# Two column blocks held in PSUM over the first rounds, modulation pieces re-spaced, small vectors prepared in steps (hybrid decoder layer, one core)

## The chip, the core and the metric

One core of a Trainium2 chip runs the whole layer as one program. The metric is the device time of one execution in microseconds (us); the time before is the median of three runs. The engines named below are PE (TensorE, matrix products), DVE (VectorE), ACT (ScalarE), POOL (GpSimd) and SP (SyncE, which here issues nearly all loads). Every engine works through its own list of instructions in order.

## What is computed

One decoder layer for 256 tokens of width 2048, in float32. Only its first third matters here:

```python
mod = silu(c) @ w_ada + b_ada            # six vectors of 2048: sh1, sc1, gt1, sh2, sc2, gt2
h = rmsnorm(x, g_mix) * (1 + sc1) + sh1
z = h @ w_in                             # 2048 x 16392; split into mq mk mv mo, mi mf, dq dk dv, sq sk sv, gm gd gs
...                                      # mLSTM, differential attention, stick-breaking attention
x = x + gt1 * (merged @ w_out)
...                                      # second norm, gated MLP with a short convolution, residual with gt2
```

`w_ada` has 2048 rows and 12288 columns. The first two of its six column groups (sh1 and sc1, 33.6 MB) must be read and summed against `silu(c)` before the matching rows of `h` exist, so the first product `h @ w_in` cannot start all of its contraction at once.

## The kernel before, in words

**Products.** Every large product splits both factors into a high part (float32r) and a low rest and adds three products: high by high, low by high, high by low. A load from `w_in` of four contraction tiles (a tile is 128 rows; `kt` counts them, 16 in all) by 512 or 440 columns lands in `raw`; ACT copies the high part (`hi`, line 320), DVE subtracts to get the low part (`lo`, line 322), both on two tiles at a time, and PE then runs the matmuls of lines 352 (orientation T, tokens on the output's partitions, two outputs) or 354 (orientation F, features on the partitions, four outputs). The other factor is `hh`/`hl`, the two parts of `h`.

**The first rounds.** Thirteen column blocks (`first`: two each for sq, sk and sv, seven of 440 columns for the gates and dq, dk, dv) are computed in rounds over the contraction, because `h` becomes ready from the front: round 1 takes kt 0 to 1 of all blocks, round 2 kt 2 to 3, round 3 kt 4 to 7, round 4 kt 8 to 11 (of eleven blocks, `NE`), and round 5 the rest. `partial` (line 467) does one block of one round. Since a block's sum does not stay in PSUM between rounds, the two PSUM accumulators (`gp`, three buffers) are emptied after each block and round: by an ACT copy in round 1 (line 476), and by a DVE multiply-add onto the sum in SBUF in all later rounds (line 478).

**The modulation.** `ada_first` makes the pieces of sh1 and sc1 for kt 0 to 1 and then 2 to 3, `ada_quad` those for kt 4 to 7, 8 to 11 and 12 to 15 ("quads" below). Each step loads a piece of `w_ada` and adds it, weighted with a column of `silu(c)`, to an accumulator on DVE (`ada_mac`, lines 204 and 206; a quad has 8 steps of two 128x1024 operations). When all 16 row tiles are in, `ada_sums` sums over partitions by matmuls with a column of ones into the single bank of pool `adaps` (line 222), DVE makes `b1` and `a1` (lines 225 to 227), and `make_h` makes `hh` and `hl` from the normalised x (lines 415, 370, 371).

**What sets the order.** The steps are Python generators in two queues, `ada` and `side`. `tick` (line 191) adds a rate to a counter after each block and runs that many steps, so the rates 0.5, 0.45 and 0.63 place the modulation steps between blocks; before a block that needs rows of `h` that are not there yet, line 469 runs steps until they are. The framework's scheduler then orders each engine's list; `issue_after` adds an ordering constraint. SP's loads are one such list. Quads, `ada_first` and four-tile weight loads share the three buffers of `rawp`; two-tile weight loads use three buffers of `adap`. Pool `mx` has four PSUM banks, used here by `norm_x` for transposes at the start and by the attention steps from block 6 of round 5 on (line 808).

```python
    rates["ada"] = 0.5
    for ci in range(13):
        partial(ci, 0, 2)
    rates["ada"] = 0.45
    for ci in range(13):
        partial(ci, 2, 4)
    with tc.issue_after(state["load"].ins):
        late_vectors()
    rates["ada"] = 0.63
    for ci in range(13):
        partial(ci, 4, 8)
    for ci in range(NE):
        partial(ci, 8, 12)
    drain(ada)
```

**Small vectors.** `late_vectors` (line 135) loads 14 small pieces (gains, convolution taps, gate biases, lambda vectors; SP, lines 140 to 151), transposes them on PE into columns and works out lambda on DVE and ACT; here it stands as one piece between rounds 2 and 3. At the start, `silu(c)` and five bias and gain vectors are transposed into one bank `pc` (lines 116 and 117) and copied to `colsA`; `norm_x` (line 388) takes the square root of the mean square (line 393) and scales and transposes x.

Of the kernel before, what the change touches and what calls it, by code (L numbers as in the profile page):

```python
# [17 lines left out]
P = 128  # L18
# [3 lines left out]
KD = D // P  # L22
# [17 lines left out]
def kernel(  # L40
# [32 lines left out]
    def sidewide(name):  # L73
        return tmp.tile([P, 512], F32, tag="sidewide", name=name, bufs=4)
# [4 lines left out]
    V, A, T = nc.vector, nc.scalar, nc.tensor  # L79
# [32 lines left out]
    nc.scalar.dma_start(rowsA[16:48], b_rows[0:32])  # L112
    nc.scalar.dma_start(rowsA[48:80], b_rows[48:80])
    V.tensor_tensor(csig, csig, crow, ALU.mult)
    pc = bank("pc")
    T.transpose(pc[:, 0:KD], csig, ident[:KD, :KD])
    T.transpose(pc[:, KD:KD + 80], rowsA, ident[:80, :80])
    colsA = const.tile([P, KD + 80], F32, name="colsA")
    V.tensor_copy(colsA[:, 0:KD], pc[:, 0:KD])
    V.tensor_copy(colsA[:, KD:KD + 80], pc[:, KD:KD + 80])  # L120
    ccol, gmix_c = colsA[:, 0:16], colsA[:, 16:32]
    bsh1_c, bsc1_c, bsh2_c, bsc2_c = (colsA[:, 32 + 16 * i:48 + 16 * i] for i in range(4))
# [12 lines left out]
    def late_vectors():  # L135
        rows = slot(3, "rows2")
        rowsB, rowsC = rows[0:27, 0:P], rows[0:64, P:2 * P]
        rowsD = rows[0:NF, 2 * P:5 * P].rearrange("k (j p) -> k j p", j=3)
        ld = nc.sync.dma_start
        ld(rowsB[0:16], g_ffn[0].rearrange("(k p) -> k p", p=P))  # L140
        ld(rowsB[16:24], g_mout[0].rearrange("h (k p) -> (h k) p", p=P))
        ld(rowsB[24:25], g_dsub)
        for r in range(2):
            ld(rowsB[25:26, r * 64:(r + 1) * 64], g_dq)
            ld(rowsB[26:27, r * 64:(r + 1) * 64], g_dk)
        ld(rowsC, w_mconv[0].rearrange("j (k p) -> (j k) p", p=P))
# [12 lines left out]
        V.tensor_scalar(gdq_c, gdq_c, 64.0 ** -0.5, None, ALU.mult)

        lp = rows[0:1, 896:1024].rearrange("o (v d) -> o v d", v=2)
        V.tensor_tensor(lp, lamv[:, 0::2, :], lamv[:, 1::2, :], ALU.mult)
        ls = const.tile([1, 2], F32, name="ls")
        V.tensor_reduce(ls, lp, AX.X, ALU.add)
        A.activation(ls, ls, AF.Exp)
        nl = const.tile([1, 1], F32, name="nl")
        V.scalar_tensor_tensor(nl, ls[:, 1:2], -LAM_INIT, ls[:, 0:1], ALU.add, ALU.subtract)
        plam = bank("plam")
        T.matmul(plam[:, 0:1], lhsT=ones[0:1, :], rhs=nl, start=True, stop=True)
        V.tensor_copy(nlam, plam[:, 0:1])  # L170

# [14 lines left out]
    def drain(queue):  # L186
        pump(queue, 1 << 30)
# [42 lines left out]
    def ada_first(k0):  # L230

        accs = [adap.tile([P, 512], F32, tag="acc", name="acc", bufs=2)]
        if k0 == 0:
            accs.append(sidewide("acc2"))
        for q in range(4):
            raw = rawp.tile([P, 4, 512], F32, tag="raw", name="raw")
            step = 2 if k0 == 0 and q == 3 else 4
            for j in range(0, 4, step):
                for i in range(2):
                    r0, c0 = q * 512 + j * P, i * D + k0 * P  # L240
                    with tc.issue_after(state["load"].ins) if k0 else nullcontext():
                        load = nc.sync.dma_start(raw[:, j:j + step, i * 256:(i + 1) * 256],
                                                 w_ada[r0:r0 + step * P, c0:c0 + 256].rearrange("(k p) f -> p k f", p=P))
            if k0 == 0:
                state["load"] = load
            with tc.issue_after(state["first"].ins) if k0 == 2 and q == 0 else nullcontext():
                ada_mac(accs, raw, 4 * q, 4)
            yield
        ada_sums(accs, k0, 2)
# [75 lines left out]
            los.append(lo)  # L325
        return his, los

    def gemm(orient, act, W, row0, col0, n, kt0, kt1, hold=None, hold_all=False):

        acc = [gp.tile([P, 512], F32, tag="gp", name="gp") for _ in range(2)]
        ah, al = act
        started, left = set(), {}
        nt = 2 if orient == "T" else n // P
        per = 1 if orient == "T" else 2

        def mms(t, ks, s0, wh, wl):
            if orient == "T":
                o, sl = acc[t][:, :n], slice(t * P, (t + 1) * P)  # L340
            else:
                o, sl = acc[t // 2][:, (t % 2) * S:(t % 2 + 1) * S], slice(t * P, (t + 1) * P)
            for w, acts in ((wh, (ah, al)), (wl, (ah,))):
                for k in ks:
                    wk = w[k // 2][:, k % 2, :]
                    for a in acts:
                        b = t // per
                        start = b not in started
                        started.add(b)
                        kw = dict(start=start, stop=s0 + k == kt1 - 1 and w is wl, skip_group_check=True)  # L350
                        if orient == "T":
                            T.matmul(o, lhsT=a(s0 + k)[:, sl], rhs=wk[:, :n], **kw)  # L352
                        else:
                            T.matmul(o, lhsT=wk[:, sl], rhs=a(s0 + k), **kw)  # L354

        for s0 in range(kt0, kt1, 4):
            nk = min(4, kt1 - s0)
            r0 = row0 + s0 * P
            wh, wl = weights(W[r0:r0 + nk * P, col0:col0 + n], nk, n, hold if s0 > kt0 or hold_all else None)
            last = s0 + nk >= kt1  # L360
            for ks in ([range(nk)] if last else [range(k0, k0 + 2) for k0 in range(0, nk, 2)]):
                for t in range(nt):
                    mms(t, ks, s0, wh, wl)
            if not last:
                tick()
        return acc
# [87 lines left out]
    first = []  # L454
# [9 lines left out]
    def shaped(src, dst):  # L464
        return src.rearrange("p (a b) -> p a b", a=dst.shape[1]) if len(dst.shape) == 3 else src

    def partial(ci, kt0, kt1):
        orient, col0, n, dest, scale = first[ci]
        while state["h"] < kt1:
            pump(ada, 1)  # L470
        pin = kt0 == 0 and ci == 1
        acc = gemm(orient, hact, w_in, 0, col0, n, kt0, kt1, hold=state["first"] if pin else None, hold_all=pin)
        for b in range(2):
            for cs, d in dest(b):
                if kt0 == 0:
# [24 lines left out]

    def stick():
# [502 lines left out]
```

## Time and profile before

| | |
|---|---|
| median of three runs | 1848.84 us (1844.38 to 1850.06) |
| the profiled execution | 1845.87 us, of which the span from the first to the last instruction is 1844.2 us |
| PE, busy share of the span | 97% |
| PE weight loads | 92% |
| DVE | 71% |
| ACT | 48% |
| mean granted TensorE clock | 0.989 of full speed |
| bytes read from HBM | 419.68 MB |

The span is what the profile's stretches are counted in, from its own start; the time of an execution is 1.7 us longer. A busy PE may still run at half the clock or wait a little between matmuls, so the count of matmuls and their pace say more than the share.

### The profile page before, as it was taken

The numbers are of one execution on the slowest core, as the hardware profiler recorded it, in microseconds if no ns is written. First come the engines' busy times: TensorE is split into PE (matmuls) and PEld (weight loads), VectorE is DVE, ScalarE is ACT, GpSimd is POOL, SyncE is SP. The second block draws the span as 40 slices with busy tenths as digits, with TensorE's granted clock in tenths as the row PEclk, the third lists the DMA queues.
The fourth block names the chain that finished last, engine by engine and source line by source line (L and its number), as shares of the span: only waits on it lengthen the run. The fifth ranks groups of instructions, "written<-read, shape, count | busy, mean of one in ns | idle before, by whom it ended". The sixth has DMA issues, their size and how long they took to land.

```text
span 1844.2 us, 30193 instructions
## 1 busy us (share of the span) xinstructions
PE 1795.0 (97%) x12461; PEld 1689.7 (92%) x12461; DVE 1313.8 (71%) x1715; ACT 878.8 (48%) x1132; POOL 9.0 (0%) x30
## 2 busy tenths in 40 slices
PE   6979899999999999999999999999999999999998
PEld 5879889999978999999999889999998899999987
DVE  6988777888888587786887576777775545555554
ACT  7533334667455554543444464444443334444432
POOL 0000000000000000000000000000000000000000
PEclk9989899999999999999999999999999999999999
DMA  9978765666677567677887547777765555555563
GB/s 331 334 256 296 252 230 167 238 240 229 231 247 266 173 218 259 209 244 271 294 307 268 188 151 240 250 241 274 251 206 197 191 185 184 182 184 183 192 217 114
DMA packets 219655, 423.73 MB, mean 230 GB/s; under 512 B 8768, under 2 KB 31613, under 8 KB 219005
## 3 DMA queue, kind: packets, MB, share of 16 engines
q1 hardware_dynamic: 217693, 417.56, 67.1%
q8 instruction: 97, 1.59, 0.4%
q10 hardware_dynamic: 1280, 2.14, 0.3%
q0 software_dynamic: 544, 2.11, 0.3%
q14 instruction: 41, 0.34, 0.0%
HBM read 419.68 MB, written 2.10 MB: 229 GB/s over the span
## 4 chain that ended last, share of the span: by engine, by line
PE 92%; DVE 4%; DMA 2%; ACT 1%; issue 1%; SPq 0%; DVEq 0%; ACTq 0%
PE gp L354 60%; PE gp L352 28%; DVE lo L322 1%; DMA raw<-in_w_in_dram 1%; DMA raw<-in_w_ada_dram 1%; DVE quads L206 1%; PE psc L602 0%; DMA x<-in_x_dram 0%; ACT hi L320 0%; PE pxt L402 0%; ACT x L396 0%; PE px L910 0%; PE pr L299 0%; PE pm L212 0%; PE pdt L587 0%
## 5 line engine op out<-in xcount | busy, mean ns | idle before, releaser
L322 DVE TENSOR_TENSOR lo<-raw,hi 128x1024 fp32r<-128x1024 f32 (+1 forms) x608 | 728.6, 1207 | 367.6 <-ACT hi L320 345.5
L320 ACT CAST hi<-raw 128x1024 fp32r<-128x1024 f32 (+1 forms) x608 | 622.3, 1038 | 740.5 <-PE gp L354 393.0
L354 PE MATMUL gp<-hh,hi 128*128 128x256 f32 x2688 | 700.7, 286 | 21.3 <-ACT hh L370 18.1
L354 PE MATMUL gp<-hl,hi 128*128 128x256 f32 x2688 | 700.8, 285 | 0.2 <-DVE hl L371 0.2
L354 PEld LDWEIGHTS gp<-hh,hi 128*128 128x128 f32 x2688 | 520.2, 194 | 23.7 <-ACT hh L370 18.3
L354 PEld LDWEIGHTS gp<-hl,hi 128*128 128x128 f32 x2688 | 520.8, 194 | 0.9 <-DVE hl L371 0.5
L354 PE MATMUL gp<-hh,lo 128*128 128x256 f32 x2688 | 511.0, 284 | 0.5 <-DVE lo L322 0.5
L354 PEld LDWEIGHTS gp<-hh,lo 128*128 128x128 f32 x2688 | 406.9, 193 | 1.4 <-DVE lo L322 0.9
L206 DVE SCALAR_TENSOR_TENSOR acc<-araw,colsA,acc 128x512 f32<-128x512 f32 x240 | 179.0, 746 | 5.2 <-DMA araw<-in_w_ada_dram 3.2
L352 PE MATMUL gp<-hi,hh 128*128 128x440 f32 (+1 forms) x416 | 157.7, 379 | 4.1 <-DVE dq L478 1.7
L352 PE MATMUL gp<-hi,hl 128*128 128x440 f32 (+1 forms) x416 | 156.3, 376 | 0.0
L352 PE MATMUL gp<-hi,atl 128*128 128x512 f32 x352 | 136.9, 389 | 0.0
L352 PE MATMUL gp<-hi,ath 128*128 128x512 f32 x352 | 136.9, 389 | 0.0
L352 PE MATMUL gp<-lo,hh 128*128 128x440 f32 (+1 forms) x416 | 113.6, 376 | 0.0
L352 PE MATMUL gp<-lo,ath 128*128 128x512 f32 x352 | 105.7, 389 | 0.0
L352 PEld LDWEIGHTS gp<-hi,hh 128*128 128x128 f32 x416 | 78.2, 188 | 16.8 <-issue 5.2
L352 PEld LDWEIGHTS gp<-lo,hh 128*128 128x128 f32 x416 | 77.8, 188 | 11.0 <-issue 1.0
L352 PEld LDWEIGHTS gp<-hi,hl 128*128 128x128 f32 x416 | 78.2, 188 | 9.8
L352 PEld LDWEIGHTS gp<-lo,ath 128*128 128x128 f32 x352 | 66.1, 188 | 13.8
L352 PEld LDWEIGHTS gp<-hi,ath 128*128 128x128 f32 x352 | 66.1, 188 | 13.7
L352 PEld LDWEIGHTS gp<-hi,atl 128*128 128x128 f32 x352 | 66.1, 188 | 13.7
L206 DVE SCALAR_TENSOR_TENSOR quads<-raw,colsA,quads 128x1024 f32<-128x1024 f32 x45 | 57.5, 1278 | 12.3 <-DMA raw<-in_w_ada_dram 12.2
(332 smaller groups left out, 1584.8 us busy)
## 6 DMA issues: line engine op xcount, KB each, us to landing
raw<-in_w_in_dram SPq DMA_DIRECT2D x98, 1024.0 KB, 5.3
raw<-in_w_up_dram SPq DMA_DIRECT2D x88, 1024.0 KB, 5.0
araw<-in_w_ada_dram SPq DMA_DIRECT2D x128, 512.0 KB, 5.3
raw<-in_w_down_dram SPq DMA_DIRECT2D x44, 1024.0 KB, 5.0
raw<-in_w_ada_dram SPq DMA_DIRECT2D x62, 512.0 KB, 5.7
raw<-in_w_branch_dram SPq DMA_DIRECT2D x24, 1024.0 KB, 6.6
raw<-in_w_in_dram SPq DMA_DIRECT2D x21, 880.0 KB, 4.8
raw<-in_w_out_dram SPq DMA_DIRECT2D x16, 1024.0 KB, 4.9
```

The source lines that it names most:

```text
L206: V.scalar_tensor_tensor(acc, raw[:, k, :], ccol[:, kt:kt + 1], acc, ALU.mult, ALU.add)
L320: A.copy(hi[:, :, :n], raw[:, k0:k0 + 2, :n])
L322: state["split"] = V.tensor_tensor(lo[:, :, :n], raw[:, k0:k0 + 2, :n], hi[:, :, :n].bitcast(F32), ALU.subtract)
L352: T.matmul(o, lhsT=a(s0 + k)[:, sl], rhs=wk[:, :n], **kw)
L354: T.matmul(o, lhsT=wk[:, sl], rhs=a(s0 + k), **kw)
```

## The change

1. **Kept sums.** Blocks 0 and 1 (sq) get two banks each of pool `mx` in round 1 and accumulate in them through all five rounds; ACT copies them out once, at the end of round 5. `gemm` takes the accumulators as an argument.
2. **Rates.** The `ada` rate is 0.56 in rounds 1 and 2, 0.75 in round 3 and 0.86 in round 4.
3. **Small vectors in steps.** `late_vectors` has three `yield`s, runs from the `side` queue with rate 0.4 from round 3 on, uses the bank of `adaps` for its transposes and for lambda, and is no longer ordered behind a load.
4. **Start.** A one-element square root (`root`) stands ahead of the squares of x; `silu(c)` has a bank and a tile of its own (`ccol`) and is copied before the other vectors are transposed; `ada_first(0)` uses one accumulator in place of two.

```diff
+    root = const.tile([P, 1], F32, name="root")
+    A.activation(root, eps_c, AF.Sqrt)
+    pc, pg = bank("pc"), bank("pg")
     T.transpose(pc[:, 0:KD], csig, ident[:KD, :KD])
-    T.transpose(pc[:, KD:KD + 80], rowsA, ident[:80, :80])
...
+    V.tensor_copy(ccol, pc[:, 0:KD])
+    T.transpose(pg[:, 0:80], rowsA, ident[:80, :80])
...
+        yield
+        pv = adaps.tile([P, 512], F32, tag="adaps", name="pv")
...
+        yield
+        plam = adaps.tile([P, 512], F32, tag="adaps", name="plam")
...
-        if k0 == 0:
-            accs.append(sidewide("acc2"))
...
-    def gemm(orient, act, W, row0, col0, n, kt0, kt1, hold=None, hold_all=False):
+    def gemm(orient, act, W, row0, col0, n, kt0, kt1, hold=None, hold_all=False, acc=None):
+        started = set() if acc is None or kt0 == 0 else {0, 1}
+        if acc is None:
+            acc = [gp.tile([P, 512], F32, tag="gp", name="gp") for _ in range(2)]
...
+        if kt0 == 0 and ci < 2:
+            kept[ci] = [bank("kept"), bank("kept")]
...
+                if ci in kept:
+                    if kt1 == KD:
+                        A.activation(d, shaped(acc[b][:, cs], d), AF.Copy, scale=scale)
+                elif kt0 == 0:
...
-    rates["ada"] = 0.5
+    rates["ada"] = 0.56
     for ci in range(13):
         partial(ci, 0, 2)
-    rates["ada"] = 0.45
     for ci in range(13):
         partial(ci, 2, 4)
-    with tc.issue_after(state["load"].ins):
-        late_vectors()
-    rates["ada"] = 0.63
+    side.append(late_vectors())
+    rates["side"] = 0.4
+    rates["ada"] = 0.75
     for ci in range(13):
         partial(ci, 4, 8)
+    rates["ada"] = 0.86
     for ci in range(NE):
         partial(ci, 8, 12)
     drain(ada)
+    drain(side)
```

DVE at the end of round 3, before. `dv..<-gp` are the last blocks' multiply-adds, `quads` the modulation steps, `b1`/`a1` the results of the partition sums for kt 8 to 11, and `hl` the low part of `h` without which round 4 cannot go on.

```order
L478 SCALAR_TENSOR_TENSOR dv_255<-gp_1645,dv_255 128x440
L322 TENSOR_TENSOR lo_1762<-raw_1755,hi_1761 128x1024
L206 SCALAR_TENSOR_TENSOR quads_257<-raw4_1815,colsA_122,quads_257 128x1024
L478 SCALAR_TENSOR_TENSOR dv_255<-gp_1682,dv_255 128x440
L206 SCALAR_TENSOR_TENSOR quads_257<-raw4_1815,colsA_122,quads_257 128x1024
L478 SCALAR_TENSOR_TENSOR dv_255<-gp_1683,dv_255 128x440
L225 TENSOR_TENSOR b1_131<-pm_1720,colsA_122 128x4
L226 TENSOR_TENSOR a1_130<-pm_1720,colsA_122 128x4
L322 TENSOR_TENSOR lo_1825<-raw_1822,hi_1824 128x1024
L227 TENSOR_TENSOR a1_130<-a1_130,colsA_122 128x4
L322 TENSOR_TENSOR lo_1829<-raw_1822,hi_1828 128x1024
L371 TENSOR_TENSOR hl_135<-ht_1732,hh_134 128x256
```

Here `b1` comes after the last block of the round (`gp_1682`, `gp_1683`). The same engine and place in the change:

```order
L231 TENSOR_TENSOR b1_135<-pm_1542,colsA_127 128x4
L232 TENSOR_TENSOR a1_134<-pm_1542,colsA_127 128x4
L326 TENSOR_TENSOR lo_1626<-raw_1623,hi_1625 128x2x440
L326 TENSOR_TENSOR lo_1630<-raw_1623,hi_1629 128x2x440
L233 TENSOR_TENSOR a1_134<-a1_134,colsA_127 128x4
L489 SCALAR_TENSOR_TENSOR dk_253<-gp_1575,dk_253 128x440
L326 TENSOR_TENSOR lo_1666<-raw_1663,hi_1665 128x2x440
L489 SCALAR_TENSOR_TENSOR dk_253<-gp_1576,dk_253 128x440
L176 COPY nlam_133<-plam_1618 128x1
L212 SCALAR_TENSOR_TENSOR quads_256<-raw4_1699,ccol_124,quads_256 128x1024
L326 TENSOR_TENSOR lo_1670<-raw_1663,hi_1669 128x2x440
L376 TENSOR_TENSOR hl_139<-ht_1554,hh_138 128x256
```

Now `b1` stands before the multiply-adds of block 9 (`gp_1575`), and `hl` three blocks ahead of the round's last one; the copy of lambda (`nlam`) lies between.

DVE at the end of round 2 in the change, the sums for kt 4 to 7; `gp_1026` and `gp_1027` are the round's last block:

```order
L233 TENSOR_TENSOR a1_134<-a1_134,colsA_127 128x4
L489 SCALAR_TENSOR_TENSOR dv_254<-gp_999,dv_254 128x440
L326 TENSOR_TENSOR lo_1051<-raw_1048,hi_1050 128x1024
L489 SCALAR_TENSOR_TENSOR dv_254<-gp_1000,dv_254 128x440
L326 TENSOR_TENSOR lo_1055<-raw_1048,hi_1054 128x1024
L163 TENSOR_SCALAR cols_131<-cols_131 128x1
L164 TENSOR_SCALAR cols_131<-cols_131 128x1
L212 SCALAR_TENSOR_TENSOR quads_256<-raw4_1021,ccol_124,quads_256 128x1024
L489 SCALAR_TENSOR_TENSOR dv_254<-gp_1026,dv_254 128x440
L489 SCALAR_TENSOR_TENSOR dv_254<-gp_1027,dv_254 128x440
L376 TENSOR_TENSOR hl_139<-ht_978,hh_138 128x256
```

The sums are made earlier here too, but `hl` is written only after the round's last multiply-add.

SP's loads near the start of the change, with what each waits for (`DMAHW0` to `DMAHW7` are eight landing counters that the loads take in turn, so a load that waits for one waits for an earlier load to land). `raw_322` is the first modulation load for kt 2 to 3, `raw2_365` the weights of the fourth block, the `rows2` loads seven of the 14 small vectors:

```order
L246 DMA raw_322<-in_w_ada_dram 128x4x256 [waits DMAHW5_49]
L143 DMA rows2_1236<-in_g_ffn_dram 16x128 [waits DMAHW6_49,PE_49,Activation_49]
L144 DMA rows2_1236<-in_g_mout_dram 8x128 [waits DMAHW7_49]
L145 DMA rows2_1236<-in_g_dsub_dram 1x128 [waits DMAHW0_49]
L147 DMA rows2_1236<-in_g_dq_dram 1x64 [waits DMAHW1_49]
L148 DMA rows2_1236<-in_g_dk_dram 1x64 [waits DMAHW2_49]
L147 DMA rows2_1236<-in_g_dq_dram 1x64 [waits DMAHW3_49]
L148 DMA rows2_1236<-in_g_dk_dram 1x64 [waits DMAHW4_49]
L319 DMA raw2_365<-in_w_in_dram 128x2x512 [waits DMAHW5_49,DVE_49]
L246 DMA raw_397<-in_w_ada_dram 128x4x256 [waits DMAHW6_49]
```

Before, all 14 stood between rounds 2 and 3 and `raw_370`, the load of that fourth block, followed the modulation loads at once. Now thirteen of them stand in two batches (seven, shown, and six behind the next two modulation loads) ahead of the fifth block's weights, and one before them.

## Rows read from the trace of the kernel before

**Rows 1.** The page, part 1: busy time of each engine.
```profile
PE 1795.0 (97%) x12461; PEld 1689.7 (92%) x12461; DVE 1313.8 (71%) x1715; ACT 878.8 (48%) x1132; POOL 9.0 (0%) x30
```
**Rows 2.** Stretches (us): length, busy PE, PEld, DVE, ACT, POOL, clock, DMA share, GB/s.
```profile
26.30:67.00 40.70, 40.68 (x242) 38.71 (x243) 36.22 (x46) 28.53 (x51) 0.00 (x0) 0.93 1.01 345
67.00:107.30 40.30, 35.41 (x200) 30.16 (x198) 39.59 (x60) 11.49 (x13) 0.00 (x0) 1.00 0.83 283
107.30:114.45 7.15, 0.00 (x1) 0.00 (x1) 6.11 (x10) 5.82 (x9) 0.00 (x0) 0.71 0.99 327
114.45:186.90 72.45, 72.26 (x424) 67.97 (x424) 59.64 (x75) 23.93 (x28) 0.00 (x0) 0.96 0.84 283
186.90:193.63 6.73, 0.01 (x1) 0.00 (x0) 5.92 (x10) 3.92 (x7) 0.00 (x0) 0.64 0.81 275
193.63:256.10 62.47, 62.47 (x376) 58.88 (x376) 51.10 (x63) 22.41 (x26) 0.00 (x0) 0.96 0.77 266
256.10:260.35 4.25, 0.04 (x1) 0.00 (x0) 2.27 (x8) 1.93 (x5) 0.00 (x0) 0.62 0.78 256
```
**Rows 3.** Who PE waited for: us in total, times, longest.
```profile
PE gp L354 <- ACT hh L370: 18.1, 3, 7.2
```
**Rows 4.** Short stretches after the first and the third wait, columns as in rows 2.
```profile
116.00:120.00 4.00, 4.00 (x20) 4.00 (x20) 1.83 (x4) 0.63 (x2) 0.00 (x0) 0.50 0.99 331
260.00:264.00 4.00, 3.65 (x17) 3.65 (x18) 1.52 (x4) 1.82 (x6) 0.00 (x0) 0.51 0.60 225
```
**Rows 5.** The chain that ended last: start, us, what; PE's pace.
```profile
796.52 51.83 PE gp L354 x432
1369.58 130.57 PE gp L352 x576
```
**Rows 6.** Timeline of PE: start, us, what; two successive matmuls of 440 columns.
```profile
102.75 0.36 PE L352 MATMUL gp<-hi,hh 128*128 128x440 f32 x1
102.95 0.36 PE L352 MATMUL gp<-hi,hl 128*128 128x440 f32 x1
```
**Rows 7.** DVE by form, 20 to 260 us: count, busy, mean ns, idle before.
```profile
L206 DVE SCALAR_TENSOR_TENSOR quads<-raw,colsA,quads 128x1024 f32<-128x1024 f32 x45 | 57.5, 1278 | 12.3 <-DMA raw<-in_w_ada_dram 12.2
L322 DVE TENSOR_TENSOR lo<-raw,hi 128x1024 fp32r<-128x1024 f32 x40 | 48.0, 1218 | 5.3 <-ACT hi L320 5.2
L478 DVE SCALAR_TENSOR_TENSOR sqT<-gp,sqT 128x512 f32<-128x512 f32 x12 | 8.2, 686 | 6.0 <-PE gp L354 6.0
L371 DVE TENSOR_TENSOR hl<-ht,hh 128x256 fp32r<-128x256 f32 x10 | 3.9, 421 | 1.3 <-ACT hh L370 1.3
```
**Rows 8.** Timeline of SP's loads: the fourth block's, then the small ones.
```profile
25.27 0.37 SPq L315 DMA_DIRECT2D raw<-in_w_in_dram  x1
...
90.10 0.47 SPq L140 DMA_DIRECT2D rows<-in_g_ffn_dram  x1
...
98.42 0.25 SPq L151 DMA_DIRECT2D rows<-in_lam_k_dram  x1
```
**Rows 9.** Loads, 0 to 300 us: KB each, median us from issue to landing.
```profile
raw<-in_w_in_dram SPq DMA_DIRECT2D x18, 1024.0 KB, 5.2
rows<-in_w_mconv_dram SPq DMA_DIRECT2D x1, 32.0 KB, 2.2
```
**Rows 10.** Timeline of the start: start, us, what, idle before and its releaser.
```profile
10.97 1.28 ACT L393 ACT_TABLE_LOAD   x1
17.96 5.39 DVE L206 SCALAR_TENSOR_TENSOR acc<-raw,colsA,acc 128x512 f32<-128x512 f32 x8 [0.26 <-DMA raw<-in_w_ada_dram]
24.01 1.23 DVE L322 TENSOR_TENSOR lo<-raw,hi 128x1024 fp32r<-128x1024 f32 x1 [0.66 <-ACT hi L320]
26.32 1.01 PE L354 MATMUL gp<-hh,hi 128*128 128x256 f32 x3 [1.63 <-ACT hh L411]
```

More of the change, by code (lines that the diff above doesn't have):

```diff
@@ L114 @@
     V.tensor_tensor(csig, csig, crow, ALU.mult)
-    pc = bank("pc")
+    root = const.tile([P, 1], F32, name="root")
+    A.activation(root, eps_c, AF.Sqrt)
+    pc, pg = bank("pc"), bank("pg")
     T.transpose(pc[:, 0:KD], csig, ident[:KD, :KD])
-    T.transpose(pc[:, KD:KD + 80], rowsA, ident[:80, :80])
[L118 to L122, printed above, removed]
+    ccol = const.tile([P, KD], F32, name="ccol")
+    V.tensor_copy(ccol, pc[:, 0:KD])
+    T.transpose(pg[:, 0:80], rowsA, ident[:80, :80])
+    colsA = const.tile([P, 80], F32, name="colsA")
+    V.tensor_copy(colsA, pg[:, 0:80])
+    gmix_c = colsA[:, 0:16]
+    bsh1_c, bsc1_c, bsh2_c, bsc2_c = (colsA[:, 16 + 16 * i:32 + 16 * i] for i in range(4))
     for b_c in (bsc1_c, bsc2_c):
@@ L167, in late_vectors @@
         V.scalar_tensor_tensor(nl, ls[:, 1:2], -LAM_INIT, ls[:, 0:1], ALU.add, ALU.subtract)
-        plam = bank("plam")
+        yield
+        plam = adaps.tile([P, 512], F32, tag="adaps", name="plam")
         T.matmul(plam[:, 0:1], lhsT=ones[0:1, :], rhs=nl, start=True, stop=True)
@@ L326, in weights @@
         return his, los
-    def gemm(orient, act, W, row0, col0, n, kt0, kt1, hold=None, hold_all=False):
-        acc = [gp.tile([P, 512], F32, tag="gp", name="gp") for _ in range(2)]
+    def gemm(orient, act, W, row0, col0, n, kt0, kt1, hold=None, hold_all=False, acc=None):
+        started = set() if acc is None or kt0 == 0 else {0, 1}
+        if acc is None:
+            acc = [gp.tile([P, 512], F32, tag="gp", name="gp") for _ in range(2)]
         ah, al = act
-        started, left = set(), {}
         nt = 2 if orient == "T" else n // P
@@ L471, in partial @@
         pin = kt0 == 0 and ci == 1
-        acc = gemm(orient, hact, w_in, 0, col0, n, kt0, kt1, hold=state["first"] if pin else None, hold_all=pin)
+        if kt0 == 0 and ci < 2:
+            kept[ci] = [bank("kept"), bank("kept")]
+        acc = gemm(orient, hact, w_in, 0, col0, n, kt0, kt1, hold=state["first"] if pin else None, hold_all=pin,
+                   acc=kept.get(ci))
         for b in range(2):
             for cs, d in dest(b):
-                if kt0 == 0:
+                if ci in kept:
+                    if kt1 == KD:
+                        A.activation(d, shaped(acc[b][:, cs], d), AF.Copy, scale=scale)
+                elif kt0 == 0:
                     A.activation(d, shaped(acc[b][:, cs], d), AF.Copy, scale=scale)
@@ L481 @@
     NE = 11
+    kept = {}
     quads = slot(4, "quads")
```

1 line of the change is left out of this document (removed).

## The prediction

> **What bounds the kernel now.** I read the busy shares first: PE is busy for 97% of the span [rows 1], so only the places where it stands or runs slowly can give anything. The stretches by round show them [rows 2]: from 26.30 us (first product) to 260.35 us (first matmul of round 5) PE stands for about 23 us, and nearly all of that is three gaps, 107.30 to 114.45, 186.90 to 193.63 and 256.10 to 260.35. The view of who waited for whom names one cause for the three: the next round's matmuls wait for `hh`, 18.1 us in total [rows 3]. After each gap PE comes back at the lower of its two clocks: 0.50 of full speed, 1.2 GHz, at 116 to 120 us and 0.51 at 260 to 264 [rows 4]. The mean clock of 0.96 in rounds 3 and 4 costs 0.04 x 72.45 = 2.9 us and 0.04 x 62.47 = 2.5 us, and 0.49 x 3.65 = 1.8 us fall into the start of round 5 [rows 2, 4]. So the gaps and their clock are worth 18.1 + 7.2 = 25.3 us.
>
> What rounds 3 and 4 would need of PE alone: a matmul of 256 columns takes 51.83 / 432 = 0.120 us, one of 512 takes 130.57 / 576 = 0.227 us [rows 5], one of 440 takes 0.20 us from start to start [rows 6]. Per contraction tile the 13 blocks are 48, 12 and 42 of these: 5.8 + 2.7 + 8.4 = 16.9 us. Round 3 (four tiles) needs 67.5 us, and round 4, two blocks of 440 fewer, 57.9 us. Measured less the clock it was 69.5 and 60.0 us, so 2 us in each are small losses that I leave in.
>
> Rounds 1 and 2 are different. DVE is busy 36.22, 39.59 and 6.11 of 88.15 us there, 81.9 in all, and the loads run at 345 GB/s in the first half [rows 2]. There DVE and the loads are the bound, not PE.
>
> **The change part by part.**
>
> *Kept sums.* Four DVE multiply-adds of 0.686 us [rows 7] fall away in each of rounds 2 to 5, four ACT copies move from round 1 to round 5, where PE is the bound and ACT has room. In round 2 this is 2.7 us of a bound engine, in round 3 also 2.7; in rounds 4 and 5 it is worth nothing, since PE covers it.
>
> *Rates and order.* No work is added; it moves forward. For kt 8 to 11 and for kt 12 to 15 the sums stand in the change's order three and more blocks before the round ends (a block of round 3 is some 5 us of PE), so I take the second and the third gap, 6.7 + 4.2 us, and their clock, 2.5 + 1.8 us, as gone. For kt 4 to 7 this is not so: `hl` comes after the last multiply-add of round 2. DVE's work up to it, against before: 4 multiply-adds fewer (2.7), two `lo` of 1.22 us later (2.4), one quad operation of 1.28 us more [rows 7], so 3.8 us less. Rows of DVE overlap a little (in these rounds their sum is 6% over the busy time), so 3.6: 81.9 - 3.6 = 78.3 us.
>
> *Small vectors.* They leave the gap between rounds 2 and 3, where SP spent 90.10 to 98.67 us on issuing them [rows 8], but they go to the start, where every load counts. The fourth block's weights were issued at 25.27 us [rows 8]. In the change seven small loads stand before them, and the counters make each wait for a load eight issues earlier; the last of these is a modulation load that lands one queue's depth after its issue, 5 us as the big loads show [rows 9]. I put the fourth block's load 2 us later and, behind the second batch of six, the fifth block's load 4 us later. DVE, in order, also waits for the lambda loads (`rows2`, line 167) and for an exponential on ACT that needs a table load of 1.28 us [rows 10]. Below, this costs nothing if DVE's waits there only fall on waits that it has anyway; above, see the second rival. DVE stood idle for 88.15 - 81.9 = 6.2 us in rounds 1 and 2; I take 2 us more, near the lower end, because PE has over 2 us of spare time per block in round 1 and DVE catches up only on what the loads leave.
>
> A rule speaks against this part. The Trainium skill, "DMA: Bandwidth & Descriptors", section "Rules for kernel authors", says that many small transfers should be made into one, since below 64 KB a transfer is mostly overhead. By it these loads cost the same wherever they stand; the trace agrees as to size, 2.2 us to landing for 32 KB against 5.2 for 1 MB [rows 9].
>
> *Start.* The table load of 1.28 us ahead of the square root goes off the path of x [rows 10]. But the path to the first matmul runs through the modulation sums: their last eight operations wait for their load at 17.96 us and end at 23.35 [rows 10], and the load queue is full until then, so an earlier x gives nothing. In the change's order the first `lo` (1.23 us) stands before the last of these operations, and only 4 in place of 8 matmuls follow. `lo` needs ACT's first `hi` and started at 24.01 before; with ACT 1.3 us earlier but the weights landing no earlier I let it start at 23.1, and the first matmul comes at 26.9 instead of 26.32 [rows 10]: 0.6 us lost.
>
> *The sum.* Round 3 starts at 26.9 + 78.3 + 8.2 + 0.4 (for the first `hl` [rows 7]) = 113.8 us. In round 3, DVE's work from the first `hl` to the last multiply-add is: before 59.64 + 5.92 = 65.6 us [rows 2]; 4 quad operations more (5.1), 4 `hl` more (1.7), 4 multiply-adds fewer (2.7) give 4.1, less the overlap 3.9: 69.5 us. PE needs 69.5 with its small losses, and the loads, 12.6 MB of weights and 9.75 steps of 1.05 MB, 66 us at 345 GB/s. Three demands this close do not fit into one another fully: I take 72 us. Round 4 takes PE's 60.0. Round 5 starts at 113.8 + 72 + 60 = 245.8 us, 14.5 us earlier, and 1.8 us of clock are saved in it. From there to the end PE is the bound as before and the work is the same. 1845.87 - 16.3 = 1829.6, rounded to **1830 us**. The profiled execution lies 3 us below the median of the runs, 1848.84, and within their spread; I leave the forecast at its level. The bounds of the unknown terms (idle of rounds 1 and 2 from 5 to 12 us, round 3 from 69.5 to 77) give the case's own range of 1823 to 1839.
>
> **The rivals.**
>
> *The gaps become many small waits.* If round 3's loads run at the 283 GB/s of before [rows 2], because three buffers feed quads and weights, its 22.8 MB take 80.6 us: round 5 starts at 254.4, 5.9 us earlier, and with the clock 1838 us. For it: DVE waited 12.3 us for quad loads [rows 7]. Against it: 345 GB/s in round 1 [rows 2], and that round 3 was PE's before, so its loads had time. 0.18.
>
> *The small loads at the start strangle the queue* (slower). Before, the batch held SP for 8.6 us [rows 8] and the next big load landed some 5 us later [rows 9]. If each of the two batches empties the queue like that, while DVE stands at the lambda product, the cost is 2 x 13.7 = 27.4 us in place of the 2 counted: 1855 us. It decides from 16.3 + 2 us on. Against it: seven issues of 0.25 to 0.5 us fit largely into a pause that SP made before 25.27. 0.06.
>
> *It doesn't do what it says.* If the loads, not the order, set all round ends (the bytes are the same), round 5 starts where it did and only its clock is saved: 1844 us. Against it: DVE and DMA were both below 0.85 busy in rounds 3 and 4 [rows 2]. 0.08.
>
> *All of it comes.* Idle of 3 us in rounds 1 and 2, round 3 at PE's 69.5, round 4 at 58.5: round 5 starts at 26.9 + 78.3 + 3 + 0.4 + 69.5 + 58.5 = 236.6, and 1845.87 - 23.8 - 1.8 gives 1820 us. 0.10.
>
> **How the numbers follow.** The forecast has the remaining 0.58. About 0.3%, 5.5 us, is what a measurement can tell from no change, so faster means below 1843. The forecast, the full gain and nearly all of the small waits are faster, 0.58 + 0.10 + 0.16 = 0.84; no change is 0.08 + 0.02 = 0.10; slower is 0.06. The range runs from just under the full gain to the case that the change doesn't work, 1818 to 1844, and leaves out the slower one and the tails.
>
> **What would show it.** Right: PE's waits for `hh` of line 370 (375 after) fall from 18.1 us to below 5, what is left stands at the start of round 3 near 114 us; first matmul near 27 us, round 5's first matmul near 246 us; no stretch at half clock at the starts of rounds 4 and 5; the rest of the span unchanged. The small loads show as a dip of the DMA rate near 28 to 32 us and no longer near 97. Wrong: a first matmul of round 3 beyond 118 us would say that the start's small loads or DVE's wait for lambda were mis-sized; many PE waits for `lo`, `hi` or multiply-adds in round 3 would say that the loads took over; a change of more than 3 us behind 260 us would say that the rest of the program's order moved too.

## The result and the profile after

The changed kernel takes **1831.07 us** (median of four runs, 1828.42 to 1836.43) against 1847.62 us (1844.38 to 1850.06) for the kernel before in the same comparison: ratio 0.9915, 95% interval 0.9887 to 0.9943. The profiled execution takes 1832.0 us, its span 1830.3 us, 13.9 us less than before. Executions of one kernel differ by some us, and those of the changed kernel also in their mean clock (0.995 at 1828.42 us, 0.992 at 1836.43).

Page, part 1 (answers to [rows 1]):

```profile
PE 1792.1 (98%) x12453; PEld 1685.4 (92%) x12453; DVE 1305.8 (71%) x1699; ACT 878.3 (48%) x1133; POOL 9.5 (1%) x30
```

Stretches by round, columns as in [rows 2], then two short ones that answer to [rows 4]:

```profile
28.59:68.00 39.41, 36.68 (x213) 34.11 (x214) 33.02 (x46) 24.19 (x45) 0.00 (x0) 0.96 0.99 334
68.00:110.80 42.80, 39.60 (x226) 34.45 (x224) 41.80 (x57) 16.36 (x22) 0.00 (x0) 0.96 0.90 322
110.80:114.92 4.12, 0.52 (x4) 0.30 (x3) 4.12 (x9) 0.60 (x3) 0.00 (x0) 0.83 0.38 105
114.92:188.60 73.68, 72.64 (x425) 67.53 (x425) 64.39 (x82) 27.60 (x36) 0.00 (x0) 0.96 0.90 306
188.60:248.60 60.00, 60.00 (x377) 56.53 (x377) 48.76 (x64) 26.27 (x33) 0.00 (x0) 1.00 0.82 275
...
116.00:120.00 4.00, 4.00 (x21) 4.00 (x21) 2.95 (x4) 1.76 (x2) 0.00 (x0) 0.50 0.99 328
260.00:264.00 4.00, 4.00 (x36) 4.00 (x35) 3.05 (x3) 1.84 (x3) 0.00 (x0) 1.00 0.40 144
```

Of the three gaps two are gone: rounds 4 and 5 follow at once, at 188.60 and 248.60 us, at full clock. The first is down from 7.15 to 4.1 us, and after it the clock is still 0.50. Who PE waited for (answers to [rows 3]):

```profile
PE pm L228 <- DVE acc L212: 3.9, 1, 3.9
PE kept L359 <- DVE hl L376: 3.6, 1, 3.6
PE gp L359 <- ACT skT L487: 2.3, 1, 2.3
```

The 18.1 us for `hh` (line 370 before, 375 now) no longer stand there at all. The 3.6 us for `hl` are what is left ahead of round 3; timelines of DVE and PE at that place:

```profile
110.95 1.21 DVE L326 TENSOR_TENSOR lo<-raw,hi 128x1024 fp32r<-128x1024 f32 x1
...
112.21 1.27 DVE L212 SCALAR_TENSOR_TENSOR quads<-raw,ccol,quads 128x1024 f32<-128x1024 f32 x1
113.40 1.13 DVE L489 SCALAR_TENSOR_TENSOR dv<-gp,dv 128x440 f32<-128x440 f32 x2
114.45 1.08 DVE L376 TENSOR_TENSOR hl<-ht,hh 128x256 fp32r<-128x256 f32 x3
```

```profile
110.82 0.50 PE L359 MATMUL kept<-hh,hi 128*128 128x256 f32 x2
114.92 0.58 PE L359 MATMUL kept<-hl,hi 128*128 128x256 f32 x1 [3.60 <-DVE hl L376]
```

Two products run, then PE stands until DVE turns to `hl`, which comes behind a `lo`, a modulation step and round 2's last two multiply-adds. These two account for 114.45 - 113.40 = 1.05 us of the wait. The start answers to [rows 10], first DVE with ACT's first `hi` behind it, then PE with the matmuls of the same sums in the kernel before (line 222) behind it:

```profile
15.04 8.63 DVE L212 SCALAR_TENSOR_TENSOR acc<-raw,ccol,acc 128x512 f32<-128x512 f32 x11 [0.19 <-DMA raw<-in_w_ada_dram]
23.58 1.22 DVE L326 TENSOR_TENSOR lo<-raw,hi 128x1024 fp32r<-128x1024 f32 x1
24.72 0.74 DVE L212 SCALAR_TENSOR_TENSOR acc<-raw,ccol,acc 128x512 f32<-128x512 f32 x1
...
22.30 1.04 ACT L324 CAST hi<-raw 128x1024 fp32r<-128x1024 f32 x1
```

```profile
25.52 1.87 PE L228 MATMUL pm<-ones,acc 128*128 128x1 f32 x8 [3.90 <-DVE acc L212]
28.59 1.22 PE L359 MATMUL kept<-hh,hi 128*128 128x256 f32 x4 [1.21 <-ACT hh L416]
...
22.74 1.95 PE L222 MATMUL pm<-ones,acc 128*128 128x1 f32 x16 [0.38 <-DVE acc L206]
```

The first product comes at 28.59 us, 2.3 later than before. SP's small loads, first and last of the first batch, the fourth block's weights, and the last of the second batch (answers to [rows 8]):

```profile
21.58 0.34 SPq L143 DMA_DIRECT2D rows<-in_g_ffn_dram  x1
...
26.52 0.22 SPq L148 DMA_DIRECT2D rows<-in_g_dk_dram  x1
28.06 0.39 SPq L319 DMA_DIRECT2D raw<-in_w_in_dram  x1
...
32.18 0.22 SPq L154 DMA_DIRECT2D rows<-in_lam_k_dram  x1
```

The dip of the loads has moved with them: from 28 to 30 us they run at 59 GB/s (before 338), from 97 to 100 us at 383 (before 41).

From round 5 to the end it takes 1830.3 - 248.6 = 1581.7 us, before 1844.2 - 260.35 = 1583.85.

### The profile page after: what moved, and what is told of

Same layout as the page of the kernel before. It is cut to its first block, busy times and chain, and to the rows that moved or that the text cites. A ratio compares the mean times of both kernels' runs of the same rounds, so it can differ in the third digit from the quotient of the medians.

```text
span 1830.3 us, 30158 instructions
## 1 busy us (share of the span) xinstructions
PE 1792.1 (98%) x12453; PEld 1685.4 (92%) x12453; DVE 1305.8 (71%) x1699; ACT 878.3 (48%) x1133; POOL 9.5 (1%) x30
## 3 DMA queue, kind: packets, MB, share of 16 engines
q1 hardware_dynamic: 217693, 417.56, 67.5%
## 4 chain that ended last, share of the span: by engine, by line
PE 92%; DVE 4%; DMA 3%; issue 1%; ACT 0%; SPq 0%; DVEq 0%; ACTq 0%
PE gp L359 57%; PE gp L357 29%; PE kept L359 2%; DMA raw<-in_w_in_dram 1%; DMA raw<-in_w_ada_dram 1%; DVE lo L326 1%; DVE quads L212 1%; DVE acc L212 1%; PE psc L615 0%; ACT hi L324 0%; PE pm L228 0%; PE px L923 0%; PE pr L303 0%; PE pdt L600 0%; PE ptf L673 0%
## 5 line engine op out<-in xcount | busy, mean ns | idle before, releaser
L359 PE MATMUL gp<-hh,hi 128*128 128x256 f32 x2560 | 664.9, 284 | 3.7 <-ACT skT L487 2.3
L359 PE MATMUL gp<-hl,hi 128*128 128x256 f32 x2560 | 663.5, 284 | 0.0
L359 PEld LDWEIGHTS gp<-hh,hi 128*128 128x128 f32 x2560 | 490.8, 192 | 5.9 <-ACT skT L487 2.5
L359 PEld LDWEIGHTS gp<-hl,hi 128*128 128x128 f32 x2560 | 490.9, 192 | 0.4
L359 PE MATMUL gp<-hh,lo 128*128 128x256 f32 x2560 | 488.2, 284 | 0.5 <-DVE lo L326 0.5
L359 PEld LDWEIGHTS gp<-hh,lo 128*128 128x128 f32 x2560 | 386.7, 192 | 1.1 <-DVE lo L326 0.7
L212 DVE SCALAR_TENSOR_TENSOR acc<-araw,ccol,acc 128x512 f32<-128x512 f32 x240 | 179.0, 746 | 5.2 <-DMA araw<-in_w_ada_dram 3.1
L357 PE MATMUL gp<-lo,hh 128*128 128x440 f32 (+1 forms) x416 | 112.6, 377 | 0.9 <-DVE lo L326 0.9
L212 DVE SCALAR_TENSOR_TENSOR quads<-raw,ccol,quads 128x1024 f32<-128x1024 f32 x45 | 57.5, 1278 | 3.7 <-DMA raw<-in_w_ada_dram 3.6
```

The costliest lines, as they stand in the source:

```text
L212: V.scalar_tensor_tensor(acc, raw[:, k, :], ccol[:, kt:kt + 1], acc, ALU.mult, ALU.add)
```

## The experiments

Twelve kernels were run in three batches of four, each batch with its own runs of the kernel before (medians 1846.27, 1846.58 and 1846.74 us). The table has, from PE's timeline, the first product and the first products of rounds 3, 4 and 5. "Goes on" is the product after a wait of 0.8 us or more, where one follows the first two products of round 3. These times are of one profiled execution each, which can lie some us from the median (e12_hl_first_old_start: 1831.16 us against 1828.86).

| kernel | first | round 3 | goes on | round 4 | round 5 | median us | ratio to before, interval |
|---|---|---|---|---|---|---|---|
| before | 26.3 | 114.5 | | 193.6 | 260.4 | 1847.62 | |
| after | 28.6 | 110.8 | 114.9 | 188.6 | 248.6 | 1831.07 | 0.9887 to 0.9943 |
| e1_no_kept | 28.6 | 116.2 | 118.1 | 193.2 | 255.2 | 1837.42 | 0.9937 to 0.9962 |
| e2_old_rates | 28.7 | 117.3 | | 197.5 | 264.4 | 1846.64 | 0.9992 to 1.0010 |
| e3_vec_held | 28.6 | 107.7 | 111.7 | 187.2 | 247.6 | 1829.16 | 0.9899 to 0.9926 |
| e4_old_start | 26.3 | 108.5 | 112.6 | 185.9 | 247.4 | 1829.36 | 0.9896 to 0.9923 |
| e5_rates_only | 26.0 | 112.5 | 115.5 | 188.2 | 250.1 | 1831.49 | 0.9908 to 0.9934 |
| e6_half_rates | 28.6 | 120.5 | | 196.8 | 256.5 | 1838.96 | 0.9944 to 0.9971 |
| e7_held_old_start | 26.1 | 106.4 | 110.3 | 186.2 | 248.0 | 1830.98 | 0.9899 to 0.9925 |
| e8_higher_rate | 26.5 | 108.0 | | 190.5 | 250.2 | 1831.47 | 0.9906 to 0.9932 |
| e9_no_kept_vec_held | 28.6 | 112.9 | 114.7 | 191.3 | 253.3 | 1837.41 | 0.9940 to 0.9963 |
| e10_no_kept_old_start | 26.3 | 112.7 | 114.6 | 187.8 | 248.5 | 1832.20 | 0.9909 to 0.9933 |
| e11_hl_first | 28.5 | 111.3 | 114.3 | 190.4 | 250.2 | 1831.65 | 0.9905 to 0.9930 |
| e12_hl_first_old_start | 26.1 | 111.5 | 112.7 | 187.1 | 247.9 | 1828.86 | 0.9887 to 0.9912 |

**One part undone at a time.** Without kept sums:

```diff
-        if kt0 == 0 and ci < 2:
+        if kt0 == 0 and ci < 0:
```

> The changed kernel (median 1831, before 1847.6) with blocks 0 and 1 emptied after every round again. Theory A, the gain is the two closed gaps ahead of rounds 4 and 5: four more multiply-adds of 0.686 us on DVE in each of rounds 2 and 3 cost at most 2.7 + 2.7 us, the gaps stay closed, 1832 to 1837. Theory B, the kept sums are what relieves DVE, and without them round 3 falls back to small waits or to a gap: 1841 or more.

With the old rates:

```diff
-    rates["ada"] = 0.56
+    rates["ada"] = 0.5
...
+    rates["ada"] = 0.45
...
-    rates["ada"] = 0.75
+    rates["ada"] = 0.63
...
-    rates["ada"] = 0.86
```

> The changed kernel with the old rates of the modulation steps (0.5, 0.45, 0.63). Theory A: the waits for hh ahead of rounds 4 and 5 come back, 9 to 12 us of them and some 4 us of low clock, less what the kept sums save on DVE: 1841 to 1847. Theory B (kept sums or the moved vectors made the gain): 1832 to 1836, waits for hh below 6 us.

With the small vectors' loads held behind the load of the moment:

```diff
-        ld = nc.sync.dma_start
+        after_load = state["load"].ins
+
+        def ld(*args):
+            with tc.issue_after(after_load):
+                nc.sync.dma_start(*args)
```

> The changed kernel with the small loads ordered behind the weights of the moment, so that they leave the start and stand late in round 2. Theory A: the fourth block's weights come 2 to 3 us earlier (issue near 25.5 us, 28.1 in the change) and DVE waits less in round 1, but SP is held some 8 us late in round 2; the two about cancel: 1829 to 1834. Theory C, the early small loads are dear (first rounds lose 5 us by them): 1824 to 1828. Theory D, taking them out of the place between rounds 2 and 3 was a main part of the gain: 1836 or more.

With the start of before:

```diff
-    A.activation(root, eps_c, AF.Sqrt)
-    pc, pg = bank("pc"), bank("pg")
+    pc = bank("pc")
...
+        if k0 == 0:
+            accs.append(sidewide("acc2"))
```

> The changed kernel with the start of before (two accumulators, one bank, no early square root). First matmul back from 28.6 to about 26.3 us. Theory A: rounds 1 and 2 are bound by DVE and loads, which start earlier by about as much, so 1 to 2.3 us are won: 1828.5 to 1830.5. Theory E: the start of round 3 is set by the loads alone and nothing moves: 1831 to 1832. Theory F: the new start is a gain of the table load's 1.28 us: 1832.5 or more.

Without the new rates nothing is left of the gain (ratio 1.0001), and the old picture is back: PE's waits, and a stretch behind the second of them:

```profile
PE kept L359 <- ACT hh L375: 14.1, 3, 7.4
```

```profile
198.00:202.00 4.00, 4.00 (x23) 4.00 (x22) 3.36 (x5) 0.94 (x3) 0.00 (x0) 0.55 0.76 268
```

So the rates carry the gain, given the rest. Undoing the kept sums costs 6.3 us, just above what theory A allowed (1832 to 1837). The early loads and the new start cost some 2 us each by the medians, as theory A had it for both, but both intervals overlap that of the whole change. Theories D and F fall, and C by 1.2 us only; E isn't told from A by the time, though the old start does bring the first product back to 26.3 us and lets round 3 go on 2.3 us earlier. The held loads of e3_vec_held do not stand late in round 2, as expected, but behind the start of round 3, and the loads run at 34 GB/s there (SP's first and last small load, and a stretch):

```profile
115.54 0.45 SPq L146 DMA_DIRECT2D rows<-in_g_ffn_dram  x1
...
122.40 0.25 SPq L146 DMA_DIRECT2D rows<-in_lam_k_dram  x1
```

```profile
120.00:124.00 4.00, 4.00 (x35) 4.00 (x35) 2.49 (x4) 3.28 (x3) 0.00 (x0) 1.00 0.16 34
```

**The rates alone, those of two rounds, and the two undone together.** The kernel before with the new rates only:

```diff
-    rates["ada"] = 0.5
+    rates["ada"] = 0.56
...
-    rates["ada"] = 0.45
...
-    rates["ada"] = 0.63
+    rates["ada"] = 0.75
...
+    rates["ada"] = 0.86
```

> The kernel before with the changed spacing of the modulation pieces alone (0.56, 0.56, 0.75, 0.86): sums of first rounds through SBUF as before, small vectors in one batch behind round 2, start as before. Theory A (the spacing by itself closes the gaps ahead of rounds 4 and 5 and shortens the one ahead of round 3; the kept sums are worth some 6 us more by freeing VectorE): 1834 to 1839 us, with waits for hh of under 6 us in all. Theory G (the spacing only fits where the kept sums have made room on VectorE first; alone it only moves VectorE's lateness to the reads of the sums): 1841 to 1846 us, with PE waiting for banks (gp) in place of hh.

After with the old rates in rounds 1 and 2:

```diff
-    rates["ada"] = 0.56
+    rates["ada"] = 0.5
...
+    rates["ada"] = 0.45
     for ci in range(13):
         partial(ci, 2, 4)
```

> The kernel after with the old spacing in rounds 1 and 2 alone (0.5 and 0.45), the new one in rounds 3 and 4 (0.75, 0.86). Theory A (each round's spacing closes the gap behind that round): the wait ahead of round 3 grows from 3.6 to 7 to 9 us while those ahead of rounds 4 and 5 stay closed: 1834 to 1840 us. Theory H (round 3's spacing is what counts, and a gap ahead of round 3 is made good later): 1829 to 1832 us.

After with both edits of e3_vec_held and e4_old_start:

```diff
+            with tc.issue_after(after_load):
+                nc.sync.dma_start(*args)
...
+            accs.append(sidewide("acc2"))
```

> The kernel after with both undone that seemed to cost at the start: two accumulators and one transpose bank as before, and the small vectors' loads held behind the load of the moment. If the two costs are separate (one at the first matmul, one at the fourth block's weights): 1825 to 1828 us. If they are one and the same lateness at the start: 1828.5 to 1831 us, no better than either alone.

And the same with a higher rate in rounds 1 and 2:

```diff
-    rates["ada"] = 0.56
+    rates["ada"] = 0.65
```

> As the run before it, and with 0.65 in place of 0.56 in rounds 1 and 2, so that the last multiply-add for k-tiles 4 to 7 comes earlier in round 2. Theory A (the 3.6 us wait ahead of round 3 and its clock are what is left of that gap): hl no longer waited for ahead of round 3, and 3 to 5 us less than the run before it: 1821 to 1826 us. Rival I (VectorE is the bound of rounds 1 and 2, and the pieces put forward push the splits and sums of these rounds back): the same as the run before it or 1 to 4 us slower, with PE waiting for lo or for a bank in round 2.

The rates alone gave 1831.49 us, 15.1 us of gain and as much as the whole change can be told to have. That is under both forecasts: theory G falls, and so does the part of theory A that added 6 us for the kept sums. In its trace, behind 100 us, PE waits for `hh` for 0.9 us, and what stands there instead is the batch of small vectors in the same gap:

```profile
PE plam L169 <- DVE nl L167: 2.2, 1, 2.2
...
PE pv L154 <- DMA rows<-in_w_mconv_dram: 1.2, 1, 1.2
PE gp L354 <- ACT hh L370: 0.9, 1, 0.9
```

Without the new rates of rounds 1 and 2 the time is 7.9 us longer. Round 3 starts at 120.5 us, where after goes on at 114.9, behind a gap that has the transposes of the small vectors in it (PE's timeline):

```profile
113.36 0.27 PE L157 MATMUL pv<-ident,rows 27*128 27x27 f32 x1 [2.06 <-issue]
...
120.53 1.22 PE L359 MATMUL kept<-hh,hi 128*128 128x256 f32 x4 [5.30 <-ACT hh L375]
```

Rounds 4 and 5 follow without a gap, as theory A had it; theory H falls. The two undone together (1830.98) are no better than either alone: the second outcome. With the higher rate round 3 begins at 108.0 us, with no wait for `hl`, and yet round 4 begins at 190.5, later than after. Rival I holds in its first form, the same time; PE's waits from 20 us on have `hi` in the place of `hl`:

```profile
PE gp L361 <- ACT hi L328: 3.3, 2, 1.7
PE kept L363 <- ACT hi L328: 2.5, 3, 2.0
```

Rival I's cause isn't shown by this, though: the held small loads go out from 119.0 to 129.3 us here, and one of the waits for `hi`, 1.9 us, ends at 135.6, behind a stretch of 109 GB/s (128 to 132 us).

**Why the kept sums pay in the changed kernel.** The rates alone need no kept sums, the changed kernel does. Without kept sums, first with the loads held, then with the old start:

```diff
+            with tc.issue_after(after_load):
+                nc.sync.dma_start(*args)
...
-        if kt0 == 0 and ci < 2:
+        if kt0 == 0 and ci < 0:
```

> The kernel after without kept sums, and with the small vectors' loads held behind the load of the moment (new spacing and new start left). The new spacing alone on the kernel before gave 1831.5 us, the kernel after without kept sums 1837.4: one of the two other parts costs 6 us where the sums aren't kept. Theory K1 (it is the small loads of the first 32 us): 1829 to 1833 us. Theory K2 (it is the start with one accumulator and two banks): 1835 to 1839 us.

```diff
+            accs.append(sidewide("acc2"))
...
-        if kt0 == 0 and ci < 2:
+        if kt0 == 0 and ci < 0:
```

> The kernel after without kept sums, and with the start of before (two accumulators, one transpose bank), the small loads left early. K1: 1834 to 1839 us. K2: 1829 to 1833 us. Both runs between 1832 and 1835 would say that each part costs some 3 us and the sum of them shows.

It is the start: K2 holds in both. With the old start the kept sums are worth 1832.20 - 1829.36 = 2.8 us by the medians, with intervals that overlap; with the new one it is 1837.42 - 1831.07 = 6.3, and with the loads held 1837.41 - 1829.16 = 8.2. Without kept sums the new start costs 5.2 us (e1_no_kept against e10_no_kept_old_start, which differ in the start alone). In their traces the delay grows on the way: 2.3 us at the first product, 3.5 where round 3 goes on, 5.4 at round 4, 6.7 at round 5. Why it grows is only half seen. e9_no_kept_vec_held, which holds the loads as well, goes on with round 3 at the same time as e10_no_kept_old_start and is still as slow as e1_no_kept. From its first product of round 3 it takes 78.4 us for the round in place of 75.1, and its loads and DVE run below those of the other from 170 to 185 us; its small loads stand in that round too (117.0 to 124.2 us). Stretches of e9_no_kept_vec_held, then of e10_no_kept_old_start:

```profile
112.91:191.29 78.38, 74.37 (x432) 67.97 (x432) 67.32 (x93) 30.41 (x41) 0.00 (x0) 0.96 0.84 287
...
170.00:185.00 15.00, 13.75 (x68) 12.01 (x67) 12.62 (x22) 8.57 (x14) 0.00 (x0) 1.00 0.70 228
```

```profile
112.70:187.78 75.08, 72.66 (x426) 67.81 (x427) 68.37 (x90) 28.97 (x38) 0.00 (x0) 0.95 0.88 302
...
170.00:185.00 15.00, 15.00 (x77) 13.81 (x76) 14.48 (x24) 7.06 (x13) 0.00 (x0) 1.00 0.87 298
```

What links the start to that dip isn't settled; the order of the weight and modulation loads on SP differs between the two as well.

**The rest of the first gap.** `hl` put ahead of the last two multiply-adds of round 2, on the changed kernel and on the one with the old start:

```diff
+                state["hl"] = state["split"] = split(hh[:, kt, :], hl[:, kt, :], t)
...
-                    V.scalar_tensor_tensor(d, shaped(acc[b][:, cs], d), scale, d, ALU.mult, ALU.add)
+                    with tc.issue_after(state["hl"].ins) if ci == 12 and kt0 == 2 else nullcontext():
+                        V.scalar_tensor_tensor(d, shaped(acc[b][:, cs], d), scale, d, ALU.mult, ALU.add)
```

> The kernel after, with the two last multiply-adds of round 2 put behind the four hl of k-tiles 4 to 7 on VectorE. Theory L (what is left of the gap ahead of round 3 is VectorE's order: hl waits behind two multiply-adds that wait for PE's last products, while its own inputs stand ready 5 us earlier): the 3.6 us wait for hl is gone and PE starts round 3 without half clock: 1825 to 1829 us. Rival M (the multiply-adds put back, or the splits, are then waited for instead): 1830 to 1833 us, with a wait for lo or a bank at the same place.

> The same on the kernel after with the start of before. Theory L: 1823 to 1828 us, 3 to 5 less than the 1829.4 us of that kernel. Rival M: 1828.5 to 1832 us.

Neither run gains what theory L asked, but neither brings `hl` forward by more than 0.6 us, so its price is not tested. On the changed kernel `hl` starts at 113.84 us in place of 114.45, and the wait falls from 3.60 to 2.54 us, by the 1.05 us of the two multiply-adds; the `lo` and the modulation step still stand ahead of `hl`. In e12_hl_first_old_start the wait is down to 0.88 us, and yet `hl` starts no earlier than with the old start alone. DVE's row for `hl` and two stretches of e4_old_start, then the same of e12_hl_first_old_start:

```profile
112.15 1.09 DVE L375 TENSOR_TENSOR hl<-ht,hh 128x256 fp32r<-128x256 f32 x3
100.00:112.00 12.00, 9.03 (x49) 7.71 (x48) 12.00 (x22) 5.67 (x10) 0.00 (x0) 1.00 0.64 209
112.00:122.00 10.00, 9.37 (x65) 9.38 (x66) 8.81 (x11) 3.68 (x5) 0.00 (x0) 0.83 0.96 333
```

```profile
112.26 1.09 DVE L375 TENSOR_TENSOR hl<-ht,hh 128x256 fp32r<-128x256 f32 x3
100.00:112.00 12.00, 11.85 (x49) 10.50 (x48) 10.87 (x20) 5.66 (x10) 0.00 (x0) 0.73 0.56 189
112.00:122.00 10.00, 8.76 (x71) 8.56 (x72) 9.95 (x13) 3.01 (x4) 0.00 (x0) 1.00 0.98 339
```

The wait is shorter because PE comes to it 2.9 us later (111.5 against 108.5 us): in this execution the half clock fell within round 2, and not behind the gap. Round 3 goes on at 112.7 us, as with the old start alone, so there was nothing to give back. The median is 0.5 us lower, inside the noise; on the changed kernel 1831.65 us shows nothing either. Both times lie where rival M put them, but its cause isn't shown: the wait of 2.0 us for `lo` in e11_hl_first comes at 180 us and not at this place. At 1828.86 us e12_hl_first_old_start is the lowest median of all, but its interval overlaps that of the changed kernel; no run here shows a kernel better than it.

## Why the prediction was right, step by step

The forecast of 1830 us is 1.1 us from the median and 2.0 from the profiled execution. The mechanism was the one named, and some terms made up for others. The profiled executions differ by 13.9 us where the sum had 16.3, the medians by 16.55, so that the median comes this close is in part luck.

- **Rates and order: right, and the main term.** Gaps 2 and 3 and their half clock are gone; e2_old_rates shows that nothing remains without the rates, e5_rates_only that they do it alone.
- **Rounds 1 and 2: right.** Foreseen were 26.9 + 78.3 + 8.2 + 0.4 = 113.8 us, so 86.9 us from the first product to round 3. Measured: 114.92 - 28.59 = 86.3, with 33.02 + 41.80 + 4.12 = 78.9 us of DVE in it, so 7.4 us of idle DVE where 8.2 were foreseen. Also right: `hl` stands behind the last multiply-add of round 2, and the half of gap 1 that this leaves.
- **Start: mis-sized.** I counted 0.6 us lost, the first product at 26.9; it is 28.59, so 2.3 us. The `lo` ahead of the last multiply-add was seen, but it starts at 23.58 and not 23.1, which is 0.5 of the 1.7 us. The larger part lies behind it: from there to the first product I allowed 26.9 - 23.1 = 3.8 us, and it took 28.59 - 23.58 = 5.0. Having half the matmuls (8 in the trace, before 16) saved nothing: all of them now wait for the last multiply-add and end at 27.39 us, 1.93 behind it. Before, the matmuls began at 22.74, ahead of the last sum, and ended 1.34 us after it. I had also taken the sums to keep their pace. With one accumulator they don't, 8.63 / 11 = 0.785 us apiece against 5.39 / 8 = 0.674 with two taking turns [rows 10], some 1.2 us over eleven; but since `hi` is only there at 23.34, this can have held up `lo` by 0.24 us at most. The parts of the start were not undone one by one.
- **Kept sums: right in size with the old start, too small with the new.** For 2.7 us in round 2, round 3 goes on 2.0 us earlier with them under the old start (e4_old_start, e10_no_kept_old_start) and 3.2 under the new one (after, e1_no_kept), and the first pair's medians are 2.8 us apart, within the noise. That the changed kernel needs them to pay for its own start (6.3 us) was no term of the sum: I added the parts as if each stood alone. Kept sums, small vectors and start together are worth 1831.49 - 1831.07 = 0.4 us on top of the rates, inside the noise.
- **Small vectors: their delay right, its price not seen.** The fourth block's load went out at 28.06 us, 2.8 later than before (2 foreseen), the fifth's at 33.75 in place of 28.41 (5.3, 4 foreseen). With the loads held into round 3 the median is 1.9 us lower; with the old start it is 1.6 us higher, so the sign isn't settled and the cost is about nothing. The Trainium skill's advice against small transfers ("DMA: Bandwidth & Descriptors", section "Rules for kernel authors") decided nothing here: moving them showed no cost that can be measured, and joining them into one wasn't tried.
- **Round 3: 72 us foreseen, 73.7 measured; round 4: 60 and 60.0.** The loads ran at 306 GB/s, between the 283 of the rival with many small waits and the 345 I hoped for.
- **Sum.** Round 5 starts at 248.6 us, not 245.8: 1.7 us from the start, 1.7 from round 3, and 0.6 back in rounds 1 and 2. The end is 2.15 us shorter behind that, 1.8 foreseen.

The rival "all of it comes" had round 3 at 69.5 us, and it took 73.7. In the changed kernel loads (0.90 of that stretch), DVE (64.39 of 73.68 us) and PE's own need (67.5) all lie near its length; which of the three decides wasn't separated. Nor does what is won ahead of round 3 all arrive at round 4: with the new rates and either the old start or kept sums, round 3 runs on from anywhere between 108.0 and 115.5 us, but round 4 begins only from 185.9 to 190.5. Part of that is the small vectors. The three kernels that run on earliest (e3_vec_held, e7_held_old_start, e8_higher_rate: 108.0 to 111.7) are those whose small loads stand in round 3. With the loads left early, e4_old_start keeps its lead on the changed kernel: 2.3 us where round 3 goes on, 2.7 at round 4 and 1.2 at round 5.

## What to carry to other kernels

Where PE stands at round ends for work that another engine does in order, look first at where that work is placed: four numbers of spacing gave all of a gain that four edits shared. Test the parts of a bundle singly and against each other, since an edit can pay only for what its neighbour costs. And before closing a last short wait, see in the trace whether the awaited work really came earlier, and what the stretch behind it waits for: here no kernel that started round 3 earlier than the changed one ended earlier by more than the noise.

## What the runs showed of the hardware

A chain of DVE multiply-adds on 128x512, each reading the sum that the one before it wrote, takes 0.785 us apiece (8.63 us for eleven); with two sums taking turns it is 0.674 (5.39 us for eight, [rows 10]). The busy time of one is 0.75 us in both kernels. Two accumulators thus take 14% off the time of such a chain.

The granted clock can fall in the middle of a round without a long wait. Stretches of the kernel after:

```profile
86.00:89.00 3.00, 1.65 (x6) 0.97 (x6) 3.00 (x4) 0.93 (x1) 0.00 (x0) 1.00 0.33 63
89.00:92.00 3.00, 2.31 (x6) 2.13 (x7) 3.00 (x7) 0.93 (x1) 0.00 (x0) 0.61 1.04 399
```

The longest wait for another engine there is 1.13 us, and PE was busy 1.65 of the 3 us before; the mean of 0.61 says that most of the second stretch ran at 1.2 GHz. In the kernel before, the same two stretches read:

```profile
86.00:89.00 3.00, 1.67 (x9) 1.23 (x7) 3.00 (x5) 1.03 (x2) 0.00 (x0) 1.00 0.95 329
89.00:92.00 3.00, 2.63 (x12) 2.20 (x13) 3.00 (x5) 0.00 (x0) 0.00 (x0) 1.00 0.95 328
```

PE's busy share was as low there, with a longer wait (1.70 us) and with the loads going on, and it kept its full clock. The two kernels do different work at that place. But e4_old_start and e12_hl_first_old_start do nearly the same from 96 to 104 us, and their clocks part too (e4_old_start first):

```profile
96.00:100.00 4.00, 3.04 (x22) 2.61 (x20) 4.00 (x8) 0.93 (x1) 0.00 (x0) 1.00 1.05 383
100.00:104.00 4.00, 4.00 (x24) 3.72 (x23) 4.00 (x9) 0.93 (x1) 0.00 (x0) 1.00 0.85 310
```

```profile
96.00:100.00 4.00, 3.04 (x20) 2.65 (x18) 4.00 (x8) 0.93 (x1) 0.00 (x0) 0.94 1.05 383
100.00:104.00 4.00, 4.00 (x14) 3.74 (x14) 3.41 (x8) 0.93 (x1) 0.00 (x0) 0.50 0.86 302
```

PE is busy for the same 3.04 us, then does 24 matmuls in one kernel and 14 in the other. What makes the difference isn't settled by these rows; e12_hl_first_old_start comes to round 3 2.9 us later.
